# A kernel of two transformer blocks: who forms the weights' sums of a seven-product multiplication, what has precedence between the products, and which tiles are multiplied in that way

## The chip, the cores and the metric

The kernel runs on one core of a Trainium2 chip. The metric is the device time of one execution in microseconds (us), the median of several runs. Engines are named as in the profile: PE is TensorE (PEld its weight loads), DVE is VectorE, ACT is ScalarE, POOL is GpSimd, SP is SyncE, which here issues the loads of the weights.

## The reference, cut to what matters

Two blocks follow each other on 512 tokens of width 1024. The first block (latent attention, a gated convolution, a gated MLP) is not touched. The second has two layers; each ends with the same MLP, of hidden width 4096, and these two MLPs are what the change touches:

```python
D_FF_2 = 4 * D_MODEL          # 4096

def _sqrelu_mlp(h, w1, w2):
    u = jax.nn.relu(h @ w1)
    return (u * u) @ w2

for i in range(DEPTH_2):      # 2
    ...                       # retention in layer 0, chunk attention in layer 1
    h = h + _sqrelu_mlp(_rmsnorm(h, mlp_norm_g[i]), mlp_w1[i], mlp_w2[i])
```

All is in float32. The kernel keeps its precision by splitting each operand into a high and a low part and multiplying three times (high by high, low by high, high by low).

## The kernel before, in words

**Tiles.** Activations lie feature by token, 128 features by 512 tokens to a tile. An MLP has 32 hidden tiles, worked on in 4 groups of 8 (`mlp`, L1080; `group`, L1092). A group first makes its 8 hidden tiles from `m_w1` (the up stage), then adds the 8 output tiles of `m_w2` for those 8 hidden tiles onto `xs` (the down stage, 8 tiles of 24 matmuls of 512 columns).

**Whole tiles.** `units` (L209) multiplies one hidden tile whole: 8 blocks of the contraction, three matmuls each, 24 matmuls of 512 columns. In group 0 of each MLP six tiles are made so (j from 0 to 5), since the norm of the layer's input is still being worked out beside them.

**Pairs by seven products.** All other hidden tiles are made two at a time by `Quarters.two` (L321). Two weight tiles and the activations are cut in halves, and seven products of half size stand for eight: `a11`, `a12`, `a22` of the weights themselves, `s1` to `s4` of sums of the weights. Each product (L305, matmul at L310) is 12 matmuls of 256 columns, so a pair takes 84 of them; the last, with `a22`, is kept back (`self.late`) and multiplied between the second and third product of the next pair, or in the down stage. `Quarters.prepare` (L251) forms the same sums of the activations once for each of four blocks, in tiles `q`, through a staging tile with the tag `qr`. In group 0 the pair of tiles 6 and 7 is made so, and in groups 1 to 3 all four pairs: 13 pairs in an MLP, 26 in all.

**The weights of a pair** (`Quarters.weights`, L273). The first tile comes through the ring `wr` as all weights do. The second is loaded into a tile of the tag `qr` (L279), which has two buffers and is shared with `prepare`. `total` (L282) forms four sums, in the order t1, t2, t4, t3, on POOL (L283). After each sum `parts` splits it: ACT copies the high part, DVE subtracts to get the low part (`split`, L114 and L130). The `a22` half is split last.

**Between the products of a pair.** The products accumulate in two banks. After the first product ACT copies its half bank into `u`, after the second into `v`, after the third again into `u`; a later product writes on the same half bank, and so waits for the copy: the third product (`s2`) writes where the first one's result has to be copied from. After the fifth product DVE adds `u` and a bank (`add(u, u, z)`), after the sixth `v` and a half bank.

**Order of work.** PE's instructions run in the order in which they are written. Those of the other engines are put in order when the kernel is built: each instruction has a precedence, by default its place in the program, and `tc.high_priority(offset=n)` moves it n places ahead; a queue, once built, is worked off strictly in order. Weight splits stand 80 places ahead (`HW`), a pair's sums and splits 150 (`HQ`); the copies and adds between products stand at their own place. `prompt` is a set of instructions that are exempt from being held behind a norm's last step (`queued_behind`).

Of the kernel before, what the change touches and what calls it, by code (L numbers as in the profile page):

```python
# [22 lines left out]

HW = 80
HQ = 150
N_E = (19, 11)
W_OUT = (8, 3, 5, 13, 13)
DOWN = (8, 0, 4, 10, 12)
# [34 lines left out]
def kernel(  # L63
# [7 lines left out]
    nc = tc.nc  # L71
    act, dve, pe, sp = nc.scalar, nc.vector, nc.tensor, nc.sync
# [11 lines left out]
    def pair():  # L84
        return ppool.tile([P, 2, T], F32R, tag="p", name="pair")

    def tmp(dt=F32):
        return tpool.tile([P, T], dt, tag="t", name="tmp")

    def bank(n=T):  # L90
        return psum.tile([P, n], F32, tag="b", name="bank")
# [18 lines left out]
    def add(out, a, b):  # L110
        dve.tensor_tensor(out=out, in0=a, in1=b, op=ALU.add)  # L111
# [4 lines left out]
    prompt = set()  # L116
# [12 lines left out]
    def copy(out, a):  # L129
        act.activation(out, a, AF.Copy)  # L130

    def split(dst, src, rows=slice(0, P), prompt_=False):

        copy(dst[rows, 0, :], src[rows, :])
        last = sub(dst[rows, 1, :], src[rows, :], f32(dst[rows, 0, :]))
        if prompt_:
            prompt.add(last.ins.name)
# [11 lines left out]
    def weight_tiles(pool=None):  # L149
        raw = wpool.tile([P, 8 * P], F32, tag="wr", name="wr")  # L150
        return [raw] + [(pool or wpool).tile([P, 8 * P], F32R, tag=t, name=t) for t in ("wh", "wl")]

    def load_weights(t, src, c):
        raw, hi, lo = t
        sp.dma_start(raw[:, c], src[:, c])
        with tc.high_priority(offset=HW):
            copy(hi[:, c], raw[:, c])
            prompt.add(sub(lo[:, c], raw[:, c], f32(hi[:, c])).ins.name)

    def weights(src, n=8 * P):  # L160
        t = weight_tiles()
        load_weights(t, src, slice(0, n))
        return t[1:]

    def rows(src, mt, k0=0, nk=8):
        return src[mt * P:(mt + 1) * P, k0 * P:(k0 + nk) * P]
# [9 lines left out]
    HALVES = (slice(0, T // 2), slice(T // 2, T))  # L176
# [67 lines left out]
    class Quarters:  # L244
# [28 lines left out]
        def weights(self, src, j, k):  # L273

            one = weight_tiles()
            load_weights(one, rows(src, j), slice(0, 8 * P))
            a = one[0]
            b = self.pool.tile([P, 8 * P], F32, name="qr", tag="qr", bufs=2)
            sp.dma_start(b, rows(src, k))  # L279
            a11, a12, a21, a22 = a[:, :T], a[:, T:], b[:, :T], b[:, T:]  # L280

            def total(out, x, y, op):  # L282
                nc.gpsimd.tensor_tensor(out=out, in0=x, in1=y, op=op)  # L283

            def parts(src):
                pr = pair()
                split(pr, src, prompt_=True)
                return pr[:, 0, :], pr[:, 1, :]

            with tc.high_priority(offset=HQ):  # L290
                t1, t2 = (self.pool.tile([P, T], F32, name="qs", tag="qs", bufs=2) for _ in range(2))
                t3, t4 = tmp(), tmp()
                total(t1, a21, a22, ALU.add)
                s1 = parts(t1)
                total(t2, t1, a11, ALU.subtract)
                s2 = parts(t2)
                total(t4, a12, t2, ALU.subtract)
                s4 = parts(t4)
                total(t3, a11, a21, ALU.subtract)
                s3 = parts(t3)  # L300
                a22 = parts(a22)
            hi, lo = one[1:]
            return (hi[:, :T], lo[:, :T]), (hi[:, T:], lo[:, T:]), a22, s1, s2, s3, s4
# [17 lines left out]
        def two(self, src, j, k, end_j, end_k):  # L321
            a11, a12, a22, s1, s2, s3, s4 = self.weights(src, j, k)
            x, z = bank(), bank()
            x0, x1, y0, z0 = x[:, HALVES[0]], x[:, HALVES[1]], z[:, HALVES[0]], z[:, HALVES[1]]
            u, v = tmp(), tmp()[:, HALVES[0]]
            yield from self.product(x0, a11, self.operand(0, 0), True)
            copy(u[:, HALVES[0]], x0)
            yield
            yield from self.product(z0, s1, self.operand(None, 0), True)
            copy(v, z0)  # L330
            yield
            yield from self.last()
            yield from self.product(x0, s2, self.operand(None, 1))
            copy(u[:, HALVES[1]], x0)
            yield
            yield from self.product(y0, a12, self.operand(1, 0))
            yield
            yield from self.product(z0, s4, self.operand(1, 1))
            add(u, u, z)
            end_j(u)  # L340
            yield
            yield from self.product(x0, s3, self.operand(None, 2))
            add(x1, v, x0)
            yield

            def rest():
                yield from self.product(x0, a22, self.operand(None, 3))
                end_k(x)
                yield
            self.late = [rest()]  # L350
# [278 lines left out]
    with tc.tile_pool(name="m1", bufs=1) as m1, tc.tile_pool(name="pt1", bufs=1) as ptp:  # L629
# [281 lines left out]
        out = att_out()  # L911
# [80 lines left out]
    for nh in (8, 8, 6):  # L992
# [10 lines left out]
        for mt in range(KT - 3 if last else KT):  # L1003
# [3 lines left out]
            if h0 == 0:  # L1007
                y = ffp.tile([P, T], F32, name=f"f{mt}", tag=f"f{mt}", bufs=1)
# [53 lines left out]
    nx = Next("mix0")  # L1062
    n_e.run(rest, *N_E)
    for mt in range(KT):
# [15 lines left out]
    def mlp(i, now, nxt):  # L1080
        norm, hn = now.norm, now.hn
        qpool = tc.tile_pool(name="qp", bufs=1, reuse_waits="tile")
        quarters = Quarters(hn, qpool.__enter__())
        hid = [pair() for _ in range(8)]

        def square_relu(j, ps):
            t = tmp()
            dve.scalar_tensor_tensor(out=t, in0=ps, scalar=0.0, in1=norm.r, op0=ALU.max, op1=ALU.mult)  # L1088
            act.activation(t, t, AF.Square)  # L1089
            split(hid[j], t)  # L1090

        def group(grp):  # L1092
            r0 = i * 32 + grp * 8
            if grp == 0:

                two = [(bank(), weights(rows(m_w1, r0 + j))) for j in range(2)]
                yield from together([units(ps, w, K8, hn) for ps, w in two],
                                    [lambda j=j, ps=ps: norm.then(lambda: square_relu(j, ps))
                                     for j, (ps, _) in enumerate(two)])
                for j in range(2, 6):  # L1100
                    w = weights(rows(m_w1, r0 + j))
                    ps = bank()
                    yield from units(ps, w, K8, hn)
                    norm.then(lambda j=j, ps=ps: square_relu(j, ps))
                    if j > 2:
                        quarters.prepare(j - 3, now.gname)
                    yield
                quarters.prepare(3, now.gname)
            for j in range(6 if grp == 0 else 0, 8, 2):
                yield from quarters.two(m_w1, r0 + j, r0 + j + 1, lambda u, j=j: square_relu(j, u),  # L1110
                                        lambda u, j=j: square_relu(j + 1, u))

        for grp in range(4):
            gen = group(grp)
            if grp == 0:
                norm.run(gen, *N_MLP[i])
            drain(gen)
            ends = grp == 3 and nxt is None

            def product(mt):  # L1120
                ws, ps = weights(rows(m_w2, i * KT + mt, grp * 8)), bank()
                return units(ps, ws, K8, hid), lambda: second_end(mt, ps)

            def second_end(mt, ps):
                add(xs[mt], xs[mt], ps)
                if ends:
                    final.square(xs[mt])
                elif grp == 3:
                    nxt.take(mt)


            first = together(*zip(*[product(mt) for mt in range(2)]))
            pull(first, 2)
            drain(quarters.last())
            drain(first)
            if grp == 3:
                qpool.__exit__(None, None, None)
            for mt in range(2, KT - 3 if ends else KT):
                w = weights(rows(m_w2, i * KT + mt, grp * 8))
                ps = bank()  # L1140
                drain(units(ps, w, K8, hid))
                add(xs[mt], xs[mt], ps)
                if ends:
                    final.square(xs[mt])
                elif grp == 3:
                    nxt.take(mt)
            if ends:
                finish(hid, [weights(rows(m_w2, i * KT + mt, grp * 8)) for mt in range(KT - 3, KT)])
# [197 lines left out]
    now, nx = nx, Next("mix1")  # L1346
# [224 lines left out]
```

## Time and profile before

| | us |
|---|---|
| median of 3 runs (2020.65 to 2021.87) | 2021.58 |
| the profiled execution, its own time | 2017.05 |
| span of the profiled execution, first to last instruction | 2015.2 |
| PE busy | 1952.5 |
| DVE busy | 1300.4 |
| ACT busy | 924.6 |
| POOL busy | 176.2 |

All times in the rows below are counted in us from the span's start. A row of the timeline has the start, the duration, the engine, the line of the kernel, the operation, output and inputs, the shape and how many like instructions are merged in it; what stands in brackets is the idle time of the engine ahead of it and what ended that time. The first MLP lies at 1030 to 1400, the second at 1630 to 2015. Matmuls are pipelined, so their pace is read from starts, not from durations.

### The profile page before, as it was taken

How to read it: one execution, taken by the hardware profiler on the slowest of the kernel's cores; microseconds unless marked ns; L12 is line 12 of the kernel's file. 1: busy time of each engine (PE TensorE's matmuls, PEld its weight loads, DVE VectorE, ACT ScalarE, POOL GpSimd, SP SyncE). 2: the span in 40 equal slices, each digit the busy share in tenths (PEclk: the TensorE clock that was granted, in tenths of full speed). 3: DMA queues.
4: the chain of work that ended last, by engine and by line, in shares of the span. 5: the costliest groups of instructions: out<-in, count | busy, mean ns of one | idle time of the engine just before them, and what ended most of it. 6: DMA issues, size and time to landing. Idle time of an engine off the chain costs nothing.

```text
span 2015.2 us, 26327 instructions
## 1 busy us (share of the span) xinstructions
PE 1952.5 (97%) x10284; PEld 1673.0 (83%) x10284; DVE 1300.4 (65%) x2238; ACT 924.6 (46%) x1571; POOL 176.2 (9%) x125
## 2 busy tenths in 40 slices
PE   9999999999999999999997999999999997999998
PEld 7787888888888888888886889898888886889897
DVE  7878953343478565446656667575698976666565
ACT  5776532232245434233444444353576754344352
POOL 1000000000000000000001224220000001324220
PEclk9999999999999999999998999999999998999999
DMA  5122233333232232323222232322322232233321
GB/s 190 58 75 76 84 94 96 104 94 94 91 115 88 85 95 80 102 74 94 74 94 84 94 105 95 108 82 90 98 88 74 71 111 77 94 109 101 105 74 63
DMA packets 59053, 185.46 MB, mean 92 GB/s; under 512 B 6928, under 2 KB 10400, under 8 KB 58928
## 3 DMA queue, kind: packets, MB, share of 16 engines
q1 hardware_dynamic: 53936, 176.02, 27.5%
q10 hardware_dynamic: 4688, 7.40, 1.2%
q8 instruction: 80, 1.31, 0.3%
q14 instruction: 45, 0.37, 0.1%
q0 software_dynamic: 304, 0.36, 0.1%
HBM read 181.56 MB, written 2.20 MB: 91 GB/s over the span
## 4 chain that ended last, share of the span: by engine, by line
issue 57%; PE 30%; DVE 6%; ACT 3%; POOL 2%; DMA 2%; SPq 0%; POOLq 0%; ACTq 0%; DVEq 0%
PE bank L169 7%; PE bank L171 7%; PE bank L170 7%; PE bank L310 6%; DVE wl L114 2%; DMA qr<-in_m_w_dram 1%; DVE pair L114 1%; POOL tmp L283 1%; ACT pair L130 1%; DVE tmp L111 1%; PE bank L526 1%; POOL qs L283 1%; ACT wh L130 1%; DVE tmp L500 0%; DVE tmp L491 0%
## 5 line engine op out<-in xcount | busy, mean ns | idle before, releaser
L169 PE MATMUL bank<-pair,wh 128*128 128x512 f32 (+1 forms) x2134 | 816.4, 383 | 0.2 <-ACT pair L130 0.2
L171 PE MATMUL bank<-pair,wh 128*128 128x512 f32 (+1 forms) x2134 | 807.6, 378 | 0.5 <-DVE pair L114 0.3
L170 PE MATMUL bank<-pair,wl 128*128 128x512 f32 (+1 forms) x2134 | 806.4, 378 | 0.0
L130 ACT ACTIVATE wh<-wr 128x1024 fp32r<-128x1024 f32 (+5 forms) x329 | 324.1, 989 | 653.2 <-PE bank L171 407.7
L114 DVE TENSOR_TENSOR wl<-wr,wh 128x1024 fp32r<-128x1024 f32 (+5 forms) x329 | 383.4, 1168 | 157.1 <-ACT wh L130 155.9
L171 PEld LDWEIGHTS bank<-pair,wh 128*128 128x128 f32 x2134 | 401.4, 188 | 77.0 <-DVE pair L114 1.7
L169 PEld LDWEIGHTS bank<-pair,wh 128*128 128x128 f32 x2134 | 401.9, 188 | 70.9 <-ACT pair L130 0.8
L170 PEld LDWEIGHTS bank<-pair,wl 128*128 128x128 f32 x2134 | 402.0, 188 | 70.4 <-DVE wl L114 0.5
L114 DVE TENSOR_TENSOR pair<-tmp,pair 128x512 fp32r<-128x512 f32 (+1 forms) x208 | 171.2, 830 | 63.7 <-ACT pair L130 60.7
L130 ACT ACTIVATE pair<-tmp 128x512 fp32r<-128x512 f32 (+1 forms) x240 | 149.8, 628 | 130.7 <-POOL tmp L283 54.8
L310 PE MATMUL bank<-q,pair 128*128 128x256 f32 x1248 | 166.4, 287 | 38.8 <-ACT pair L130 26.6
L310 PEld LDWEIGHTS bank<-q,pair 128*128 128x128 f32 x1248 | 157.0, 192 | 44.2 <-ACT pair L130 27.1
L111 DVE TENSOR_TENSOR x<-x,bank 128x512 f32<-128x512 f32 (+1 forms) x99 | 66.0, 669 | 170.0 <-PE bank L171 170.0
L283 POOL TENSOR_TENSOR qs<-qr 128x512 f32<-128x512 f32 x26 | 40.9, 1573 | 1478.0 <-DMA qr<-in_m_w_dram 1478.0
L108 DVE TENSOR_TENSOR tmp<-bank,rb 128x512 f32<-128x512 f32 (+1 forms) x76 | 50.2, 666 | 103.9 <-PE bank L171 101.3
L310 PE MATMUL bank<-pair,wh 128*128 128x256 f32 x416 | 83.0, 283 | 0.0
L169 PE MATMUL bank<-wh,pair 128*128 128x512 f32 x200 | 79.3, 396 | 0.6 <-ACT tmp L130 0.6
L171 PE MATMUL bank<-wl,pair 128*128 128x512 f32 x200 | 78.0, 390 | 0.0
L170 PE MATMUL bank<-wh,pair 128*128 128x512 f32 x200 | 77.9, 390 | 0.0
L494 ACT ACTIVATE tmp<-tmp,small 128x512 f32<-128x512 f32 (+1 forms) x96 | 53.4, 556 | 34.1 <-DVE small L491 32.9
L310 PEld LDWEIGHTS bank<-pair,wh 128*128 128x128 f32 x416 | 67.8, 190 | 0.8 <-ACT tmp L130 0.2
L1089 ACT ACTIVATE tmp<-tmp 128x512 f32<-128x512 f32 x64 | 40.1, 627 | 61.1 <-DVE tmp L1088 61.1
(182 smaller groups left out, 2010.2 us busy)
## 6 DMA issues: line engine op xcount, KB each, us to landing
wr<-in_m_w_dram SPq DMA_DIRECT2D x102, 512.0 KB, 3.7
wr<-in_r_qkg_dram SPq DMA_DIRECT2D x32, 512.0 KB, 3.5
qr<-in_m_w_dram SPq DMA_DIRECT2D x26, 512.0 KB, 3.7
wr<-in_w_gate_dram SPq DMA_DIRECT2D x20, 512.0 KB, 3.5
wr<-in_w_up_dram SPq DMA_DIRECT2D x20, 512.0 KB, 3.5
wr<-in_w_down_dram SPq DMA_DIRECT2D x16, 512.0 KB, 3.4
wr<-in_r_v_dram SPq DMA_DIRECT2D x16, 512.0 KB, 3.5
wr<-in_r_out_dram SPq DMA_DIRECT2D x16, 512.0 KB, 3.7
```

The source lines that it names most:

```text
L108: dve.tensor_tensor(out=out, in0=a, in1=b, op=ALU.mult)
L111: dve.tensor_tensor(out=out, in0=a, in1=b, op=ALU.add)
L114: return dve.tensor_tensor(out=out, in0=a, in1=b, op=ALU.subtract)
L130: act.activation(out, a, AF.Copy)
L169: pe.matmul(out, lhsT=ah, rhs=bh, start=start, stop=False)
L170: pe.matmul(out, lhsT=al, rhs=bh, start=False, stop=False)
L171: pe.matmul(out, lhsT=ah, rhs=bl, start=False, stop=stop)
L283: nc.gpsimd.tensor_tensor(out=out, in0=x, in1=y, op=op)
L310: pe.matmul(out, lhsT=x[:, c], rhs=y, start=start and k + i == 0, stop=k == 3 and i == 2, skip_group_check=True)
L494: act.activation(s[:, :n], s[:, :n], AF.Exp, bias=self.mx[:, col], scale=-1.0, accum_out=self.sm[:, col])
L526: pe.matmul(o, lhsT=a, rhs=b, start=j == 0 and a is v, stop=j == NT - 1 and a is v)
L1089: act.activation(t, t, AF.Square)
```

## The change

The four sums of a pair's weights are formed by DVE instead of POOL, and stand in `prompt`. The three copies and two adds between the products stand 300 places ahead instead of at their own place. In group 0 tiles 6 and 7 are multiplied whole like the six before them; the four `prepare` steps follow tiles 2 to 5 instead of tiles 3 to 5 (three) and the end of tile 5 (the fourth).

```diff
+HP = 300
...
             def total(out, x, y, op):
-                nc.gpsimd.tensor_tensor(out=out, in0=x, in1=y, op=op)
+                prompt.add(dve.tensor_tensor(out=out, in0=x, in1=y, op=op).ins.name)
...
             yield from self.product(x0, a11, self.operand(0, 0), True)
-            copy(u[:, HALVES[0]], x0)
+            with tc.high_priority(offset=HP):
+                copy(u[:, HALVES[0]], x0)
             yield
             yield from self.product(z0, s1, self.operand(None, 0), True)
-            copy(v, z0)
+            with tc.high_priority(offset=HP):
+                copy(v, z0)
             yield
             yield from self.last()
             yield from self.product(x0, s2, self.operand(None, 1))
-            copy(u[:, HALVES[1]], x0)
+            with tc.high_priority(offset=HP):
+                copy(u[:, HALVES[1]], x0)
             yield
             yield from self.product(y0, a12, self.operand(1, 0))
             yield
             yield from self.product(z0, s4, self.operand(1, 1))
-            add(u, u, z)
+            with tc.high_priority(offset=HP):
+                add(u, u, z)
             end_j(u)
             yield
             yield from self.product(x0, s3, self.operand(None, 2))
-            add(x1, v, x0)
+            with tc.high_priority(offset=HP):
+                add(x1, v, x0)
             yield
...
-                for j in range(2, 6):
+                for j in range(2, 8):
                     w = weights(rows(m_w1, r0 + j))
                     ps = bank()
                     yield from units(ps, w, K8, hn)
                     norm.then(lambda j=j, ps=ps: square_relu(j, ps))
-                    if j > 2:
-                        quarters.prepare(j - 3, now.gname)
+                    if j < 6:
+                        quarters.prepare(j - 2, now.gname)
                     yield
-                quarters.prepare(3, now.gname)
-            for j in range(6 if grp == 0 else 0, 8, 2):
+            for j in range(8 if grp == 0 else 0, 8, 2):
                 yield from quarters.two(m_w1, r0 + j, r0 + j + 1, lambda u, j=j: square_relu(j, u),
                                         lambda u, j=j: square_relu(j + 1, u))
```

## Rows read from the trace of the kernel before

**Rows 1.** Waits of PE, whole span: total us, times, longest us.

```profile
PE bank L310 <- ACT pair L130: 26.6, 2, 13.5
PE bank L310 <- ACT tmp L130: 10.3, 12, 1.7
```

**Rows 2.** Timeline of PE, the first pair of each MLP and what follows it.

```profile
1073.06 0.28 PE L310 MATMUL bank<-pair,wh 128*128 128x256 f32 x1
...
1087.79 0.58 PE L310 MATMUL bank<-q,pair 128*128 128x256 f32 x1 [13.14 <-ACT pair L130]
...
1097.71 0.40 PE L169 MATMUL bank<-pair,wh 128*128 128x512 f32 x1
...
1673.57 0.28 PE L310 MATMUL bank<-pair,wh 128*128 128x256 f32 x1
...
1698.59 0.40 PE L169 MATMUL bank<-pair,wh 128*128 128x512 f32 x1
```

**Rows 3.** Windows: length; PE, PEld, DVE, ACT, POOL busy (instructions); granted clock; DMA; GB/s.

```profile
1052.00:1073.00 21.00, 21.00 (x95) 17.39 (x94) 16.02 (x24) 13.23 (x20) 0.00 (x0) 1.00 0.24 76
1073.00:1098.00 25.00, 11.21 (x75) 10.48 (x75) 17.34 (x23) 12.52 (x19) 7.52 (x5) 0.73 0.39 126
...
1142.00:1186.00 44.00, 42.41 (x342) 41.37 (x342) 32.78 (x42) 25.10 (x46) 13.65 (x8) 1.00 0.32 102
```

**Rows 4.** Timelines of DVE, SP and POOL before the first pair's sums.

```profile
1079.94 1.22 DVE L114 TENSOR_TENSOR q<-qr,q 128x1024 fp32r<-128x1024 f32 x1
...
1081.23 3.01 SPq L279 DMA_DIRECT2D qr<-in_m_w_dram  x2
...
1085.82 1.25 POOL L283 TENSOR_TENSOR qs<-qr 128x512 f32<-128x512 f32 x1 [1045.66 <-DMA qr<-in_m_w_dram]
```

**Rows 5.** Timeline of PE, group 1 of MLP 0; last two: group 3 of MLP 1.

```profile
1142.74 0.28 PE L310 MATMUL bank<-pair,wh 128*128 128x256 f32 x1
...
1151.33 0.28 PE L310 MATMUL bank<-pair,wh 128*128 128x256 f32 x1
...
1177.87 1.69 PE L310 MATMUL bank<-q,pair 128*128 128x256 f32 x12 [1.23 <-ACT tmp L130]
...
1183.69 0.40 PE L169 MATMUL bank<-pair,wh 128*128 128x512 f32 x1
...
1916.92 0.28 PE L310 MATMUL bank<-pair,wh 128*128 128x256 f32 x1
...
1957.51 0.40 PE L169 MATMUL bank<-pair,wh 128*128 128x512 f32 x1
```

**Rows 6.** Timeline of ACT ahead of the wait at 1177.87.

```profile
1174.19 0.63 ACT L130 ACTIVATE pair<-tmp 128x512 fp32r<-128x512 f32 x1 [3.19 <-POOL tmp L283]
...
1177.46 0.36 ACT L130 ACTIVATE tmp<-bank 128x256 f32<-128x256 f32 x1
```

**Rows 7.** Timeline of POOL: a sum by itself, and the next group's first sum.

```profile
1137.44 1.30 POOL L283 TENSOR_TENSOR tmp<-wr,qr 128x512 f32<-128x512 f32 x1
...
1170.45 1.47 POOL L283 TENSOR_TENSOR qs<-qr 128x512 f32<-128x512 f32 x1 [5.41 <-DMA qr<-in_m_w_dram]
1171.87 2.28 POOL L283 TENSOR_TENSOR tmp<-wr,qs 128x512 f32<-128x512 f32 x1
```

**Rows 8.** DVE groups by shape, window 1142 to 1186: busy us, mean ns, idle before.

```profile
L114 DVE TENSOR_TENSOR pair<-tmp,pair 128x512 fp32r<-128x512 f32 x12 | 10.8, 910 | 3.6 <-ACT pair L130 3.3
L114 DVE TENSOR_TENSOR wl<-wr,wh 128x1024 fp32r<-128x1024 f32 x5 | 7.7, 1540 | 3.6 <-ACT wh L130 3.6
L114 DVE TENSOR_TENSOR pair<-qs,pair 128x512 fp32r<-128x512 f32 x6 | 4.1, 684 | 2.0 <-ACT pair L130 2.0
```

**Rows 9.** Timeline of PE, a stretch of whole tiles, its first and 70th matmul.

```profile
1029.74 0.39 PE L171 MATMUL bank<-pair,wh 128*128 128x512 f32 x1
...
1045.38 0.39 PE L171 MATMUL bank<-pair,wh 128*128 128x512 f32 x1
```

**Rows 10.** DMA issues by line: count, KB each, us to landing.

```profile
qr<-in_m_w_dram SPq DMA_DIRECT2D x26, 512.0 KB, 3.7
```

## The prediction

> **What bounds the kernel now.** I began with the engines' busy times: PE is busy for 1952.5 of 2015.2 us, every other engine far less, so only time in which PE waits, or works at less than its pace, can be won. The waits of PE name the places: two waits at line 310 for a split by ACT, 26.6 us in all, and twelve at the same line for a copy by ACT, 10.3 us [rows 1]. Both belong to the pairs by seven products; all else is small.
>
> The timeline of PE shows the two long waits. In the first pair of each MLP the first product runs, and then PE stands for over 13 us until the second (`s1`) has its weights [rows 2]. The reason stands in three queues: the second weight tile of the pair needs a `qr` buffer, both are held by `prepare`, the subtraction that frees one begins at 1079.94 and takes 1.22, and the load is issued at 1081.23, one step later; POOL begins the first sum at 1085.82 [rows 4]. By then PE has long been idle, and its granted clock over the stretch is 0.73 of full speed, which is partly the lower of its two levels, where it is 1.00 in the stretch before [rows 3].
>
> The short waits are seen in the timelines of PE and ACT. At 1177.87 PE waits for a copy that ACT begins at 1177.46 [rows 5, 6]; the product that it copies had been done 24 matmuls before. ACT was not short of time (25.1 us busy of 44 in this stretch [rows 3]): from 1171.0 to 1174.19 it stood at a split for which POOL had no sum yet, and more such splits follow in front of the copy. POOL in turn had waited 5.41 us for the load of another pair, with a sum that could have gone first queued behind [rows 7].
>
> **The change part by part.** Paces first. Whole tiles: 69 steps from 1029.74 to 1045.38 are 0.2267 us a matmul of 512 columns [rows 9]. Products: an undisturbed first pair takes 72 matmuls from 1142.74 to 1151.33, 0.1193 us each [rows 5].
>
> *Tiles 6 and 7 whole.* The two first pairs last from 1073.06 to 1097.71 and from 1673.57 to 1698.59, 24.65 and 25.02 us [rows 2], for 72 matmuls that need 8.59. 16.1 and 16.4 us are lost, 32.5 together, the slow restart included. In their place come no products at all in group 0. The price: two whole tiles are 48 x 0.2267 = 10.88 us, a pair is 84 x 0.1193 = 10.02, so 0.86 for each MLP, +1.7. Net -30.8. The splits that feed the two whole tiles are one of 1024 columns each on ACT and DVE, and a whole tile lasts 5.44 us; the stretch before has DVE busy 16.0 and ACT 13.2 of 21 us, one `prepare` among it [rows 3]. `prepare` moves one tile ahead, and its work (a subtraction of 1.22 us and smaller ones [rows 4]) is hidden by the whole tiles; should DVE get late, the result is wanted only after group 0's down stage, eight whole tiles or 43.5 us later. SP loses the place where it stood at a `qr` buffer; the `qr` load of the first pair of group 1 finds both buffers free. What is late next there: nothing, as that pair is fed during the down stage.
>
> *Sums on DVE.* 24 pairs x 4 sums go from POOL to DVE. A subtraction of the same shape with no POOL beside it takes 0.684 us [rows 8]; a sum takes POOL 1.30 alone and up to 2.28 beside DVE [rows 7]. The chain of sums of a pair shortens from some 6 us to 4 x 0.684 = 2.7. The load of DVE: in the pair stage of group 1 it is busy 32.78 of 44 us, with eight sums on POOL [rows 3]. Eight sums add 5.5. But beside POOL its own subtractions are stretched: 12 average 0.910 and 5 large ones 1.540 [rows 8], against 0.684 and 1.22 for quiet ones of their shapes [rows 8, 4]: 12 x 0.226 + 5 x 0.32 = 4.3 comes back. So about 34.0 of the 41.7 us that the same stretch lasts once its 2.3 lost are gone: 82%, a reserve of 7.7 us in four pairs. Direct gain nothing, cost nothing as long as this reserve covers it. The Trainium skill (SBUF — State Buffer, Who interferes with whom) says that a GpSimd operation and a VectorE operation with two SBUF inputs exclude each other, the later one standing for the whole of the earlier. By that up to 8 x 1.30 = 10.4 us would come back instead of 4.3, and DVE would be at 67%; the rows show a smaller stretch on DVE and one on POOL too, and I keep 4.3.
>
> *Precedence of copies and adds.* The six pair stages last from 1142.74 to 1183.69 (40.95) for the first and from 1916.92 to 1957.51 (40.59) for the last [rows 5], the four between take 40.7 to 41.7, together 247.2. Each holds 324 matmuls, 38.65 us undisturbed. 15.3 us are lost in all, 10.3 as waits for the copies [rows 1], the rest as refilling behind them. A copy takes 0.36 [rows 6] and has two to three products' time (24 matmuls, 2.86 us) before PE needs it, so once it is not behind a split it is hidden. The ends are nothing and 15.3, and below nothing if DVE's sums make new waits (below). I take four fifths, 12.2: two causes of the waits, the order on ACT and the late sums, are both dealt with, but each queue is fixed when the kernel is built and the load of the next pair can still come late. What waits behind a copy that is now early in ACT's queue is a split; ACT has 19 us to spare in 44.
>
> *The sum.* -32.5 + 1.7 - 12.2 = -43.0 on the profiled execution's 2017.05, 1974.1. The median of the runs lies 4.5 us above that execution, and the forecast for the median is 2021.58 - 43.0 = 1978.6. With all 15.3 it is 1975.5, with half of it 1983.2.
>
> **The rivals.** *The short waits stay.* The copies may be built into the same places, or DVE, whose queue is in order, may stand at a first sum for the load of `qr` as POOL does at 1170.45, with subtractions behind it that PE needs. For it: POOL waits for that load [rows 7], and it takes 3.7 us to land [rows 10]. Against it: the reserve on DVE, and that the copies are on ACT. Then only the first part counts: 2021.58 - 30.8 = 1990.8; this is also the case in which the precedence does not do what it says.
>
> *The wait of the first pair moves to group 1.* If the loads of that pair are queued late, part of the 32.5 comes back there; with half of it, and the short waits gone, 1978.6 + 16.3 = 1995. Against it: in the kernel before, that pair starts at 1142.74 with no wait ahead of it [rows 5], though its loads came behind the late ones of group 0.
>
> *DVE becomes the bound, and the kernel slower.* If the first sum of every pair holds DVE for a whole landing, 3.7 us [rows 10], and nothing is in front of it to fill the time, the reserve of 1.9 us a pair is overdrawn by 1.8, and 24 pairs lose 43 us in place of what they lose now: 2021.58 - 30.8 + 43 = 2034, the short waits being kept. It is slower from 1.3 us a pair on. For it: DVE is the second most loaded engine, and in the pair stages the sums make it more so. Against it: two `qr` buffers, so that most loads are issued a pair ahead, and a first group of sums that falls into the down stages. The Trainium skill (Perfetto Trace Analysis, Optimizing Scalar/DVE Operations) would rather take work off a saturated VectorE, even to GpSimd, though it adds that the two share a port and that this may not help; by the first half the change goes the wrong way and this rival's time follows. The trace has DVE at 75% in the pair stage [rows 3], so not saturated, and the second half is what the stretched subtractions show.
>
> **How the numbers follow.** Forecast 0.63; the short waits stay 0.22; the wait moves 0.09; DVE the bound 0.06. The first three are all faster by far more than 0.2% (4 us, about what a measurement of this kernel can tell from no change), the last slower: faster 0.93, same 0.01, slower 0.06. The range reaches from 1974, a little under the forecast with all 15.3 us won, to 1993, which takes in the forecast's own half (1983) and the case in which the short waits stay (1990.8, with 2 us for new waits on DVE); the case of the moved wait is only partly in it, the slow one out.
>
> **What would show it.** In the waits of PE the two of 13 us are gone and no wait over 5 us stands in the MLPs; the twelve for copies are gone or short. From the first matmul of tile 6 to the down stage PE takes 10.9 us at a granted clock of 1.00. The pair stages last 38.7 to 39.5 us each. POOL is idle in the MLPs, DVE's subtractions are back at 0.69 and 1.23, and its idle time in front of the first sum, for the load of `qr`, is under 2 us a pair. I am wrong if the pair stages last 41 us or more, if DVE is busy there for over 90%, or if a long wait stands at the first pair of group 1.

## The result, and the profile after

The changed kernel takes 1974.47 us (median of 4 runs, 1974.2 to 1976.13), the kernel before 2021.12 beside it (4 runs): a ratio of 0.9776, with a 95% interval of 0.9759 to 0.9794. A second set gave 1973.43 against 2018.51, 0.9778 (0.9765 to 0.9792). The forecast was 1978.6 in a range of 1974 to 1993. The profiled executions are easier to compare step by step: the span fell from 2015.2 to 1972.5 us, by 42.7, where the sum of the terms was 43.0.

The page, busy time by engine, and the granted clock in 40 slices:

```profile
span 1972.5 us, 26036 instructions
PE 1948.5 (99%) x10212; PEld 1668.0 (85%) x10212; DVE 1289.7 (65%) x2322; ACT 914.4 (46%) x1557; POOL 9.7 (0%) x21
PEclk9999999999999999999999999999999999999999
```

PE does hardly less work than before, but is idle for 24 us of the span instead of 63. DVE has 96 operations more from the sums and is still busy 11 us less. The waits of PE at line 311 (310 before):

```profile
PE bank L311 <- DVE bank L112: 1.1, 3, 0.5
```

The 26.6 and 10.3 us of [rows 1] are gone; one small new wait is there, for DVE's add. The windows view of two stretches of MLP 0 (length; PE, PEld, DVE, ACT, POOL busy; clock; DMA; GB/s): tiles 6 and 7 and the down stage behind them, then the pair stage of group 1.

```profile
1074.92:1129.32 54.40, 54.40 (x242) 45.06 (x240) 32.27 (x43) 20.30 (x26) 0.00 (x0) 1.00 0.38 123
...
1129.32:1167.87 38.55, 38.55 (x326) 38.55 (x325) 31.07 (x48) 23.62 (x44) 0.00 (x0) 1.00 0.35 107
```

PE is busy in every microsecond of both, at the full clock. Before, the first stretch lasted 69.68 us (from 1073.06 to 1142.74, [rows 2, 5]) and the second 40.95 [rows 5]. In DVE's groups by shape, window 1128 to 1172 (busy us, mean ns), the stretching that [rows 8] showed is gone:

```profile
L115 DVE TENSOR_TENSOR pair<-tmp,pair 128x512 fp32r<-128x512 f32 x13 | 8.6, 685 | 0.1
L115 DVE TENSOR_TENSOR wl<-wr,wh 128x1024 fp32r<-128x1024 f32 x5 | 6.1, 1221 | 3.8 <-ACT wh L131 3.8
```

Where DVE stands for a load ahead of a first sum (waits of DVE: total us, times, longest):

```profile
DVE qs L284 <- DMA qr<-in_m_w_dram: 17.1, 16, 1.9
```

### The profile page after: what moved, and what is told of

The parts are those of the page before. It is cut to its first block, busy times and chain, and to the rows that moved or that the text cites. A ratio compares the mean times of both kernels' runs of the same rounds, so it can differ in the third digit from the quotient of the medians.

```text
span 1972.5 us, 26036 instructions
## 1 busy us (share of the span) xinstructions
PE 1948.5 (99%) x10212; PEld 1668.0 (85%) x10212; DVE 1289.7 (65%) x2322; ACT 914.4 (46%) x1557; POOL 9.7 (0%) x21
## 4 chain that ended last, share of the span: by engine, by line
PE 82%; DVE 10%; ACT 4%; DMA 2%; issue 2%; SPq 0%; POOLq 0%; POOL 0%; ACTq 0%; DVEq 0%
PE bank L172 25%; PE bank L170 25%; PE bank L171 24%; PE bank L311 6%; DVE pair L115 2%; DVE wl L115 2%; DMA qr<-in_m_w_dram 1%; ACT pair L131 1%; DVE tmp L112 1%; PE bank L532 1%; ACT wh L131 1%; PE bank L513 1%; ACT tmp L500 1%; DVE pt L115 1%; DVE tmp L1094 1%
## 5 line engine op out<-in xcount | busy, mean ns | idle before, releaser
L170 PE MATMUL bank<-pair,wh 128*128 128x512 f32 (+1 forms) x2166 | 829.7, 383 | 0.3 <-ACT pair L131 0.3
L172 PE MATMUL bank<-pair,wh 128*128 128x512 f32 (+1 forms) x2166 | 820.7, 379 | 0.5 <-DVE pair L115 0.3
L171 PE MATMUL bank<-pair,wl 128*128 128x512 f32 (+1 forms) x2166 | 819.3, 378 | 0.1
L115 DVE TENSOR_TENSOR wl<-wr,wh 128x1024 fp32r<-128x1024 f32 (+5 forms) x331 | 375.7, 1138 | 159.5 <-ACT wh L131 158.5
L171 PEld LDWEIGHTS bank<-pair,wl 128*128 128x128 f32 x2166 | 408.5, 189 | 72.4 <-DVE wl L115 0.9
L115 DVE TENSOR_TENSOR pair<-tmp,pair 128x512 fp32r<-128x512 f32 (+1 forms) x204 | 137.6, 686 | 17.7 <-ACT pair L131 16.0
L311 PE MATMUL bank<-q,pair 128*128 128x256 f32 x1152 | 146.3, 282 | 1.2 <-DVE bank L112 1.1
L311 PEld LDWEIGHTS bank<-q,pair 128*128 128x128 f32 x1152 | 140.7, 189 | 3.7 <-DVE bank L112 3.7
L311 PE MATMUL bank<-pair,wh 128*128 128x256 f32 x384 | 76.3, 282 | 0.0
L500 ACT ACTIVATE tmp<-tmp,small 128x512 f32<-128x512 f32 (+1 forms) x96 | 53.4, 557 | 33.4 <-DVE small L497 32.2
L112 DVE TENSOR_TENSOR tmp<-tmp 128x512 f32<-128x512 f32 (+1 forms) x90 | 56.8, 632 | 14.0 <-ACT tmp L385 13.4
```

The lines of the kernel that those rows point to most:

```text
L115: return dve.tensor_tensor(out=out, in0=a, in1=b, op=ALU.subtract)
L170: pe.matmul(out, lhsT=ah, rhs=bh, start=start, stop=False)
L171: pe.matmul(out, lhsT=al, rhs=bh, start=False, stop=False)
L172: pe.matmul(out, lhsT=ah, rhs=bl, start=False, stop=stop)
L311: pe.matmul(out, lhsT=x[:, c], rhs=y, start=start and k + i == 0, stop=k == 3 and i == 2, skip_group_check=True)
L500: act.activation(s[:, :n], s[:, :n], AF.Exp, bias=self.mx[:, col], scale=-1.0, accum_out=self.sm[:, col])
```

## The experiments

Two theories of the short waits were open (late sums, or the order on ACT), and for the long ones the ring against `prepare`'s own time. A table below puts the pair stages side by side.

### The three parts one by one

*Tiles whole, alone* (`e1_whole`): the third hunk of the change on the kernel before.

```diff
-                for j in range(2, 6):
+                for j in range(2, 8):
...
-            for j in range(6 if grp == 0 else 0, 8, 2):
+            for j in range(8 if grp == 0 else 0, 8, 2):
```

> Only tiles 6 and 7 whole; sums stay on POOL, copies at their own place. Theory (the two first pairs lost 32.5 us to the shared qr buffers, and two whole tiles cost 0.86 more than a pair): about 31 us faster than before, the two waits of 13 us gone, the twelve waits for copies (10 us recorded, 15 us of stage time) still there. Rival (the wait moves to the first pair of group 1): 16 us faster or less, with a wait of some us at 1130.

1987.1 us against 2018.62, 0.984 (0.9826 to 0.9855): 31.5 us. Waits for copies remain, 9.4 us, and no wait stands at the first pair of group 1. The first term stands as it was worked out.

*Sums on DVE, alone* (`e2_sums`): the first hunk, the sums' place in `prompt` included, which was not tested by itself.

```diff
-                nc.gpsimd.tensor_tensor(out=out, in0=x, in1=y, op=op)
+                prompt.add(dve.tensor_tensor(out=out, in0=x, in1=y, op=op).ins.name)
```

> Only the sums on DVE; tiles 6 and 7 by products, copies at their own place. Theory (the short waits have two causes, late sums from POOL and the order on ACT): the first-pair waits stay, shorter by 2 to 4 us each, and half of the 15 us of the pair stages goes: 8 to 14 us faster. Rival (order on ACT is the only cause): 2 to 6 us faster, the pair stages still at 40.5 to 41.7 us. Rival (DVE becomes the bound): pair stages of 42 us or more, slower.

2036.93 us, **slower** by 18.3 us, 1.009 (1.0075 to 1.0105). Two of PE's waits in this kernel:

```profile
PE bank L310 <- ACT pair L130: 25.1, 2, 12.6
PE bank L310 <- DVE bank L111: 23.9, 6, 4.1
```

No wait for a copy by ACT is left in this kernel (`e10_adds`, below, has such waits again with the sums as early). In their place PE waits six times, once in each pair stage, for the add of `x1`. DVE's timeline in the first of them shows why, and PE's shows the price:

```profile
1159.55 0.69 DVE L283 TENSOR_TENSOR qs<-qr 128x512 f32<-128x512 f32 x1 [2.12 <-DMA qr<-in_m_w_dram]
1160.16 0.68 DVE L111 TENSOR_TENSOR tmp<-tmp,bank 128x512 f32<-128x512 f32 x1
...
1161.96 0.69 DVE L283 TENSOR_TENSOR tmp<-wr,qs 128x512 f32<-128x512 f32 x1
1162.56 0.68 DVE L283 TENSOR_TENSOR tmp<-wr,qr 128x512 f32<-128x512 f32 x1
1163.16 0.68 DVE L283 TENSOR_TENSOR qs<-qs,wr 128x512 f32<-128x512 f32 x1
1163.77 1.31 DVE L114 TENSOR_TENSOR pair<-tmp,pair 128x512 fp32r<-128x512 f32 x2
...
1166.80 0.42 DVE L111 TENSOR_TENSOR bank<-tmp,bank 128x256 f32<-128x256 f32 x1
```

```profile
1167.27 5.49 PE L310 MATMUL bank<-q,pair 128*128 128x256 f32 x24 [4.08 <-DVE bank L111]
```

Ten operations, sums and splits of later pairs among them, stand between the add into `u` at 1160.16 and the add into the bank at 1166.80. The kept-back product writes on that bank, and PE stands for 4.08 us. DVE is not overloaded here, 32.8 us busy in the 45.7 of the stage; the two adds that PE waits for are in a bad place of its queue. The ten operations take 6.0 us. The 2.12 us for which DVE stood at a load of `qr`, just ahead of the add into `u`, have a share too, and such a stand of 1.8 to 2.2 us lies ahead of each of the six waits.

A wait costs more than its own length. The windows view of the 5.4 us behind this one, its last columns granted clock, DMA share and GB/s:

```profile
1167.20:1172.60 5.40, 5.33 (x25) 5.33 (x26) 3.40 (x6) 1.89 (x3) 0.00 (x0) 0.50 0.50 180
```

TensorE works at the lower of its two levels there; from 1155 to 1160 the granted clock was 1.00. The six stages last 37.1 us longer than those of the change: 23.9 us are the waits, and some 14 (an estimate from the granted clock of the six stages, 0.92 to 0.96) are the slower pace behind them.

*Precedence, alone* (`e3_prec`): the copies and adds 300 places ahead, on the kernel before.

> Only the precedence of copies and adds; sums on POOL, tiles 6 and 7 by products. Theory (two causes): half of the 15 us of the pair stages goes, 6 to 10 us faster, first-pair waits unchanged. Rival (late sums are the only cause): the pair stages stay at 40.5 to 41.7 us, 0 to 2 us faster. Rival (order is the only cause): the pair stages fall to 38.6 us, 15 us faster.

2021.58 us (10 runs) against 2018.62 (15 runs), 1.0013 (1.0004 to 1.0023): no gain, but 3 us lost. Waits for copies are still 8.8 us: the moved instructions are in other places, but the splits for which POOL has no sum are still in ACT's queue (ACT waits 60.8 us for POOL's sums, 73.8 before). The pair stages gain 0.4 us in all; four of the stretches behind them take 45.8 us instead of 45.0.

### Two parts of three

*Without the sums on DVE* (`e5_whole_prec`): the change with this hunk undone.

```diff
-                prompt.add(dve.tensor_tensor(out=out, in0=x, in1=y, op=op).ins.name)
+                nc.gpsimd.tensor_tensor(out=out, in0=x, in1=y, op=op)
```

> The change without the sums on DVE: tiles whole, copies and adds 300 ahead, sums on POOL. Theory now (late sums from POOL held ACT, so precedence alone gives nothing): pair stages 40 to 43 us as with the precedence alone, about 1987 us, 12 to 14 us slower than the change. Rival (precedence gives half once the first pairs are gone): about 1981 us.

1988.16 us, 0.9841 (0.9826 to 0.9855): what the whole tiles alone give. In this kernel ACT still stands at splits for POOL (waits of ACT):

```profile
ACT pair L131 <- POOL tmp L284: 35.5, 26, 4.1
```

*Without the copies' precedence* (`e10_adds`) and *without the adds'* (`e11_copies`): the change with one or the other undone.

```diff
-            with tc.high_priority(offset=HP):
-                copy(u[:, HALVES[0]], x0)
+            copy(u[:, HALVES[0]], x0)
...
```

```diff
-            with tc.high_priority(offset=HP):
-                add(x1, v, x0)
+            add(x1, v, x0)
...
```

> The change with the three copies back at their own place, only the two adds 300 ahead. Theory now (the sums on DVE end the waits for copies by themselves; of the precedence only the adds matter): as fast as the change within 3 us, pair stages 38.5 to 39 us. Rival (the prediction: the copies' place matters): waits for ACT's copies come back, pair stages 40 us or more, 8 to 14 us slower than the change.

> The change with the two adds back at their own place, only the three copies 300 ahead. Theory now (an add behind a dozen of DVE's splits and sums keeps the kept-back a22 product waiting): waits of about 4 us on DVE's add in each of the six pair stages, stages of 44 to 46 us, 30 to 40 us slower than the change, about 2007 us. Rival (the copies' place carries the gain): within 5 us of the change.

With the adds alone 1979.75 us, 0.9798 (0.9784 to 0.9813); with the copies alone 2005.78, 0.9932 (0.9915 to 0.9948). PE's waits, first of `e10_adds`, then of `e11_copies`:

```profile
PE bank L311 <- ACT tmp L131: 6.6, 10, 1.1
```

```profile
PE bank L311 <- DVE bank L112: 22.8, 6, 4.0
```

The expectation for `e10_adds` was too simple: two copies stand behind five splits on ACT again. Its timeline ahead of the longest of these waits, which ends at 1153.38:

```profile
1150.35 1.67 ACT L131 ACTIVATE pair<-tmp 128x512 fp32r<-128x512 f32 x3
...
1152.97 0.64 ACT L131 ACTIVATE tmp<-bank 128x256 f32<-128x256 f32 x2
```

This costs 9.7 us in the pair stages and some 5 us of time; part of it comes back behind the stages, where the change has a small new wait (below) and `e10_adds` has none. `e11_copies` is as expected, with a stretch at the lower clock behind each wait as in `e2_sums`. So of the precedence the adds carry some 30 us of time and the copies some 5, and both only with the sums on DVE.

| kernel | sums | copies ahead | adds ahead | six pair stages, us in all |
|---|---|---|---|---|
| before | POOL | no | no | 247.2 |
| precedence alone | POOL | yes | yes | 246.8 |
| tiles whole | POOL | no | no | 246.2 |
| tiles whole, precedence | POOL | yes | yes | 244.5 |
| sums alone | DVE | no | no | 268.4 |
| change without adds ahead | DVE | yes | no | 266.5 |
| change without copies ahead | DVE | no | yes | 241.0 |
| change | DVE | yes | yes | 231.3 |

### The first pair of an MLP

*The ring alone* (`e4_ring`): the staging of `prepare` leaves the ring `qr`; the pair 6 and 7 stays by products.

```diff
-            t = self.pool.tile([P, 4, T // 2], F32, name="qr", tag="qr", bufs=2)
+            ta, tb = (tmp().rearrange("p (a n) -> p a n", a=2) for _ in range(2))
...
-            copy(hi, t)
-            sub(lo, t, f32(hi))
+            for e, t in ((0, ta), (2, tb)):
+                copy(hi[:, e:e + 2, :], t)
+                sub(lo[:, e:e + 2, :], t, f32(hi[:, e:e + 2, :]))
```

> Only the staging of the activations' sums is moved from the qr ring into two tmp tiles, so that the pair's second weight tile finds a free qr buffer; everything else as before. Theory (the ring is the cause of the 13 us waits): the two waits fall under 3 us each, 26 to 33 us faster than before. Rival (the time that prepare's own work takes on ACT and DVE is the cause): the waits stay over 10 us, under 5 us faster.

2011.97 us, 0.9966 (0.9954 to 0.9979): 6.7 us, neither theory. The first pairs still take 22.4 and 22.0 us. PE's timeline in the first one:

```profile
1078.65 0.38 PE L311 MATMUL bank<-q,pair 128*128 128x256 f32 x1 [2.50 <-ACT pair L130]
1079.73 1.68 PE L311 MATMUL bank<-q,pair 128*128 128x256 f32 x7 [0.70 <-DVE pair L114]
1083.43 0.58 PE L311 MATMUL bank<-q,pair 128*128 128x256 f32 x1 [2.02 <-DVE q L114]
1086.77 0.79 PE L311 MATMUL bank<-q,pair 128*128 128x256 f32 x2 [2.77 <-ACT q L130]
1088.86 3.15 PE L311 MATMUL bank<-q,pair 128*128 128x256 f32 x13 [1.29 <-DVE q L114]
```

The long wait falls to 2.5 us, and behind it PE waits for `q`, the sums of the activations. The last split of `q` on DVE, first in the kernel before, then in this one:

```profile
1082.62 1.23 DVE L114 TENSOR_TENSOR q<-qr,q 128x1024 fp32r<-128x1024 f32 x1 [1.12 <-ACT q L130]
```

```profile
1088.12 1.46 DVE L114 TENSOR_TENSOR q<-tmp,q 128x512 fp32r<-128x512 f32 x2
```

In the kernel before it ends at 1083.85, 3.9 us before PE goes on at 1087.79 [rows 2]: a second cause, hidden behind the ring, but the shorter one. In `e4_ring` it ends at 1089.58. The pair's own splits, which no longer wait for the load, now stand in front of it in DVE's queue, and POOL's sums, formed at the same time, hold DVE's operations up (1.51 us instead of 0.42 for one at 1080.19). Taking away the ring uncovers the late `q` and makes it later.

*Both eased* (`e13_pair_early`): the change with pair 6 and 7 by products, `prepare` one tile earlier as in the change, and its staging out of the ring as above.

```diff
-                for j in range(2, 8):
+                for j in range(2, 6):
...
-                    if j < 6:
-                        quarters.prepare(j - 2, now.gname)
+                    quarters.prepare(j - 2, now.gname)
...
-            for j in range(8 if grp == 0 else 0, 8, 2):
+            for j in range(6 if grp == 0 else 0, 8, 2):
```

> The change, but tiles 6 and 7 by products again, with prepare one tile earlier (as in the change) and its staging in two tmp tiles, so that the qr ring is free. Theory (ring and lateness of prepare's q together made the first pair's 16 us): with both eased the first pair takes under 13 us, within 4 us of the changed kernel either way. Rival (ACT and DVE have no time left for pair 6,7 beside the norm, prepare and six tiles): the first pair takes over 18 us, 12 us or more slower than the change.

1993.74 us against 1973.43 for the change on the same chip. The first pairs take 18.4 and 17.8 us. The windows view of the stretch before and of the pair:

```profile
1052.00:1074.60 22.60, 22.60 (x103) 18.72 (x102) 20.17 (x33) 18.52 (x28) 0.00 (x0) 1.00 0.27 91
1074.61:1093.03 18.42, 13.07 (x73) 12.07 (x72) 12.16 (x21) 9.37 (x17) 0.00 (x0) 0.72 0.29 90
```

And from 1060 to the last split of `q`:

```profile
1060.00:1085.50 25.50, 20.15 (x92) 16.63 (x91) 24.53 (x43) 19.75 (x34) 0.00 (x0) 0.89 0.32 102
```

DVE is busy for 20.2 of the 22.6 us ahead of the pair, and for 24.5 of 25.5 until `q` is there: at this place the splits of six tiles, `prepare` and the pair's weights are more than it gets done in time. Multiplying the two tiles whole is the right cure for this; the two smaller ones leave 19.0 of the 32.5 us lost.

### How near DVE is to its bound, and what is left

*Each sum formed twice* (`e9_double`), on the changed kernel.

```diff
-                prompt.add(dve.tensor_tensor(out=out, in0=x, in1=y, op=op).ins.name)
+                for _ in range(2):
+                    prompt.add(dve.tensor_tensor(out=out, in0=x, in1=y, op=op).ins.name)
```

> The change with each of the four sums formed twice on DVE, some 5 us more of DVE's time in a pair stage (31.1 of 38.6 us busy now). Theory (DVE has a reserve): pair stages of 39.5 us or less, under 6 us slower than the change. Rival (DVE is already at its bound, the prediction's slow case): pair stages of 42 us and more, over 20 us slower.

1974.57 us beside 1973.43 for the change on the same chip, with overlapping intervals (0.9783, 0.9769 to 0.9796). The pair stages are unchanged to 0.2 us; DVE in the first:

```profile
1129.60:1168.14 38.54, 38.54 (x325) 38.54 (x324) 33.81 (x54) 22.73 (x41) 0.00 (x0) 1.00 0.26 80
```

At 88% of DVE's time PE still never waits in this stage. Up to there the load on DVE is not the limit.

*The kept-back product later* (`e7_late`, and again as `x_late` beside the change as `x_after`).

```diff
-            pull(first, 2)
+            pull(first, 6)
             drain(quarters.last())
```

> The change, and in the down stage the kept-back product of the last pair comes after 6 matmul groups instead of 2. Theory (at the end of each group this product waits for the add of x1 on DVE, 1.1 us recorded in three waits and 2.6 us with refilling over six groups): 1.5 to 2.6 us faster than the change, no wait of PE for DVE's bank left. Rival (these 2.6 us are not on the path): the same time as the change.

> The changed kernel once more, as the measure for the other three on the same chip: 1974 to 1976 us by every theory.

> The change with the kept-back product after 6 groups of the down stage, once more. Theory (the 2.6 us behind the waits for the add of x1 are on the path): 2 to 4 us faster than the changed kernel on the same chip. Rival (the difference seen before lay between chips): within 1 us of it.

`e7_late` 1970.74 us, 0.9756 (0.9742 to 0.9771); `x_late` 1969.27 against 1973.43 for `x_after`: 4.2 us **faster than the change**, the fastest kernel of the study. In the changed kernel, at the end of group 2, DVE and then PE:

```profile
1251.32 1.23 DVE L115 TENSOR_TENSOR wl<-wr,wh 128x1024 fp32r<-128x1024 f32 x1 [1.04 <-ACT wh L131]
...
1253.06 0.42 DVE L112 TENSOR_TENSOR bank<-tmp,bank 128x256 f32<-128x256 f32 x1
```

```profile
1253.54 1.70 PE L311 MATMUL bank<-q,pair 128*128 128x256 f32 x12 [0.43 <-DVE bank L112]
```

With the product four groups later that wait does not appear. The six stretches behind the pair stages lose 2.2 us in the change against before (the first, for example, goes from 45.03 to 45.13 us, the second to 45.72); in `x_late` the four between two pair stages are back at 45.03. Of the 3.9 us by which its profiled span is shorter than that of `x_after`, 3.1 lie in these six stretches, and 0.8 ahead of the first pair stage, where both kernels are the same.

## Why the prediction was right, and where it was not

**Tiles 6 and 7 whole: -30.8 forecast, -30.9 measured.** The two stretches from tile 6 to the pairs of group 1 fell from 69.68 to 54.40 and from 70.05 to 54.40 us. `e1_whole` by itself gives 31.5. The price of 1.7 us and the cover for `prepare` held: from 1052 to 1073 DVE is now busy for 17.0 and ACT for 16.0 us, where [rows 3] have 16.0 and 13.2, and the whole tiles wait for none of it. The wait did not move to group 1. One sentence was too short: "the reason stands in three queues" named the ring alone. `e4_ring` shows a second cause behind it, the late `q`; the number did not suffer, since whole tiles need neither.

**The pair stages: -12.2 forecast, -15.9 measured.** The step that was mis-sized is "I take four fifths". All of it went, and a little more than the 15.3 counted as lost: 38.55 us for 324 matmuls are 0.1190 each, not the 0.1193 taken.

**Where that gain comes from was seen wrongly.** The prediction booked it under the copies and adds, and the sums under "direct gain nothing, cost nothing". `e3_prec` and `e5_whole_prec` show the precedence to be worth 0 to 2 us of the stages while POOL forms the sums, and `e2_sums` the sums alone to cost 18 us. Neither part is worth its term by itself; together they are worth 15.9. I had argued from two causes of the waits ("both dealt with") but costed the parts as if they added up.

**The load of DVE: 34.0 of 41.7 us forecast, 82%; 31.07 of 38.55 measured, 81%** (33.4 of 41.6 in the stretch that was forecast, with ten sums in it instead of eight). The stretching by POOL came back as counted: 0.910 and 1.540 us went to 0.685 and 1.221. DVE's waits for the loads stay under 2 us (17.1 in 16), as the last paragraph of the prediction asked.

What the stretching is was read wrongly. POOL and DVE in the kernel before:

```profile
1159.33 1.76 POOL L283 TENSOR_TENSOR tmp<-wr,qs 128x512 f32<-128x512 f32 x1
1161.05 2.28 POOL L283 TENSOR_TENSOR tmp<-wr,qr 128x512 f32<-128x512 f32 x1
```

```profile
1160.11 2.06 DVE L114 TENSOR_TENSOR wl<-wr,wh 128x1024 fp32r<-128x1024 f32 x1 [0.18 <-ACT wh L130]
1162.09 0.67 DVE L111 TENSOR_TENSOR tmp<-tmp,bank 128x512 f32<-128x512 f32 x1
```

The split on DVE ends 1.08 us after the first sum on POOL, and takes 1.22 by itself; the second sum ends 1.16 us after the split, and takes 1.30 by itself. The trace has 146 such overlaps of a sum with a DVE operation whose two inputs both lie in SBUF, and the times of all of them are those of one that stands until the other is through: the later one ends 0.55 us (128x512 on DVE), 1.08 to 1.13 (128x1024) or 1.13 to 1.17 (a sum on POOL) after the earlier. The add at 1162.09, with one input in a bank, stands for nothing. The Trainium skill (SBUF — State Buffer, Who interferes with whom) says that two such operations exclude each other. The trace agrees with it. The 67% that the prediction drew from it do not follow: they let each sum hold DVE for its whole 1.30 us, but DVE stands only for what is left of a sum when its own operation comes. The sums on POOL are made late in the same way, by DVE's splits.

**The slow rival was the right engine, but the main mechanism was another.** It let DVE lose by its load and by standing at transfers. `e9_double` takes away the first: 88% busy and no loss. The second has a share, 1.8 to 2.2 us ahead of each wait in `e2_sums`, but in the changed kernel DVE stands at the loads as well, and PE waits for none of it in the pair stages. The slow outcome exists, 2036.93 us in `e2_sums`, mainly by order: a short add that PE waits for behind ten operations that nobody waits for yet. That this is close to the rival's 2034 is chance: the rival counts the whole tiles in, which `e2_sums` has not, and its "in place of what they lose now" does not fit its sum, which keeps the short waits. The precedence of the adds is what the change has against it. I had asked what stands behind a waiting instruction, and not what stands in front of an instruction that PE needs.

**New, and not forecast: 2.2 us at the ends of the groups.** The prediction looked for a new wait on DVE at the first sums. It came at the last pair of a group, where no next pair's products stand between `s3` and the kept-back product: two groups of the down stage, 1.4 us, must cover the add of `x1`, and in front of the adds DVE stands for ACT and splits a whole weight tile (1251.32). `x_late` shows it, by removing it. In the kernel before, the same split stands there, but the add ends at 1271.09 and the product starts at 1271.85; that PE came later there because of its short waits fits, but was not tested.

**The rest** is 1.9 us that lie before the MLPs and have another source (below). So 30.9 + 15.9 - 2.2 - 1.9 = 42.7 us, by which the span fell. That this is so near to the 43.0 forecast is luck in part: 3.7 us more in the pair stages make up for 4.1 us lost in two places that the forecast did not have.

**The median was forecast 4.1 us too high.** The 43.0 us were taken off a median that lay 4.5 us above its profiled execution; in the changed kernel the median lies 0.3 us above its own. So 1974.47 lies only 0.5 us inside the range, and the second set's 1973.43 just outside it, beside a kernel before that was 3.1 us quicker in that set than the 2021.58 from which the forecast started.

## What to carry to other kernels

When work moves to an engine that feeds the bottleneck, its load can be the smaller question: look in its queue for the short instructions on which the bottleneck waits, and what will stand in front of them. Parts of a change that meet in one queue don't add up; cost them together, or test each alone before calling one of them harmless. A long wait can hide a second one, and work that no longer stands in the first can make the second longer, so name the next late operand before promising that a freed buffer ends it.

## What the runs showed that was not expected

TensorE's clock fell behind waits of only a microsecond, in one execution and not in another of the same program. In the first block, which the change does not touch, PE waits twice between 152 and 155 us: 0.9 and 0.5 us in the changed kernel, 0.8 and 0.6 in the kernel before. The windows of 155 to 160 us, first of the changed kernel, then of the same kernel in its second set (`x_after`):

```profile
155.00:160.00 5.00, 5.00 (x22) 4.34 (x21) 4.12 (x9) 4.86 (x10) 0.00 (x0) 0.66 0.22 87
```

```profile
155.00:160.00 5.00, 5.00 (x29) 4.34 (x28) 4.48 (x11) 4.87 (x9) 0.00 (x0) 1.00 0.22 88
```

At a granted clock of 0.66, part of the stretch at the lower of the two levels, PE gets 22 instructions done instead of 29. This and a like dip at 216 to 222 us (0.72) make the changed kernel reach its first MLP 1.8 us later in one profile than in the other; the profile of the kernel before has 1.00 in both windows. `e9_double`, on the chip of `x_after`, has 0.66 in the first window again, so it is not a matter of the chip; what decides it is not shown. A kernel with many short waits has more places for this. That it is why the runs of the kernel before spread over 2015.3 to 2021.9 us, and those of the change over 1972.5 to 1976.1, fits, but was not tested. The mean granted clocks of the kernel before, on record for 31 runs beside the experiments, go with it: 0.991 in the two quickest, and 0.988 or 0.989 in all over 2018.5 us.
